# The product with w_oa in an encoder block: moved ahead of the neighbourhood attention and made of half-size products, with the modulation starting behind it

## The chip, the cores and the metric

The kernel runs on one core of one Trainium2 chip. The metric is the time of one execution on the device in microseconds; smaller is better. TensorE is called PE in the profile, VectorE DVE, ScalarE ACT, GpSimd POOL and SyncE SP. The three engines ACT, POOL and SP also start DMA transfers, each from a queue of its own that runs in order.

## The reference, cut to what matters

One layer over 512 tokens of 2048 features, all in float32:

```
mod = SiLU(c) @ w_ada + b_ada            # six vectors of 2048: shift, scale, gate, twice
h   = RMSNorm(x) * (1 + scale1) + shift1
[qA,kA,vA,qB,kB,vB,gA,gB] = h @ w_in
yA  = global attention (8 heads of 128)  # on qA, kA, vA
yB  = neighbourhood attention (8 heads)  # on qB, kB, vB
m   = sigmoid(gA) * (yA @ w_oa) + sigmoid(gB) * (yB @ w_ob)
x   = x + gate1 * (m @ w_out)
x   = x + gate2 * SwiGLU(RMSNorm(x) * (1 + scale2) + shift2)
out = RMSNorm(x)
```

w_oa and w_ob are 1024 x 2048, w_out is 2048 x 2048, w_ada is 2048 x 12288.

## The kernel before

**Split products.** Every float32 operand of a matmul is split in a high and a low half: ACT copies the high half (L163), DVE subtracts it for the low half (L165). `mm3` then issues three matmuls (L183 high x high, L184 high x low, L185 low x high). A *unit* is a weight tile of 128 x 1024 (512 KB): SP loads it into one of four `raw` buffers (L190), the two halves go to one of three `whl` buffers, and 24 matmuls with 512 columns consume it. So the loads and the splits can run up to three or four units ahead of PE.

**Two shapes of product.** `form1` (L235) computes a product with the features on the partitions, two blocks of 128 features at a time; w_in's gates, w_oa and w_ob go through it. `form2` (L249) does it with tokens on the partitions, as for the values. After each unit both call `pump` (L211), which runs due functions, one function of the list `later`, and as many steps of the background list `bg` as the current pace says.

**The modulation in the background.** The products with w_ada that only the second half of the layer needs are computed on DVE: POOL loads a tile `mw` of 128 x 1024 into one of three buffers (L335, `fetch`), and DVE multiplies it by a value of c for each partition and adds it to `acc` (L355 for the first of 16 tiles, L357 for the others). One tile is one step of `bg`. 112 tiles go this way. After 16 of them two row products on PE (bank Y and T) sum over the partitions, and DVE copies the row out (L378).

**The order around the change.** Gate A (`sg_a`) is done first; the global attention `att_a` of heads 4 to 7 (softmax chain on DVE and ACT, four transposes into bank T at L714, split pt, product into bank Y, `keep_y` stores y by ACT's queue, L684 and L685) is filled with the matmuls of the next product in program order, which is gate B, heads 0 to 8. With `p_a` released, `p_w` is taken and the modulation starts beside gate B at one step per unit. Then comes the neighbourhood attention (`att_b`) with its v, q and k, then the rest of gate B, during which `attended` loads and splits the sixteen y, one per unit (`yr`, by SP). Last comes the loop over eight pairs of feature blocks: the product of yA with w_oa (two units), evacuated by `gated` (L847, times the gate loaded by SP; for the first twelve of `sg_a` the sigmoid is taken here), the product with w_ob (two units), the sum (L859) and the split into `mT`, which w_out takes. The list `paces` gives each unit of this loop its modulation steps.

**Seven products for eight.** `group7` computes a 2 x 2 block product with seven half-size products in place of eight: the weights are loaded as two tiles, four sums of 128 x 512 are formed on DVE (`wforms`, L1008 to L1011), and four splits give the halves of seven combinations; 256 columns per matmul; seven banks are combined on DVE at the end. Before the change it is used in the feed-forward part only, with the pool `wq` adding one `raw` and two `whl` buffers.

## Time and profile before

| | us |
|---|---|
| runs (3): median, lowest, highest | 2488.75, 2488.61, 2493.84 |
| profiled execution, its own time | 2481.72 |
| span of the profiled execution | 2480.0 |
| PE busy in the span | 2449.8 (99%) |
| DVE busy | 1883.9 (76%) |
| ACT busy | 1027.6 (41%) |
| heads 4 to 7 of the global attention, with gate B's first matmuls | about 365 to 412 |
| first load of the modulation | 412.6 |
| loads of the sixteen y | about 781 to 826 |

The span runs from the first to the last instruction; the execution's own time is 1.72 us longer. In a row of a view the columns are the start, the duration, the engine, the line, the operation, the tile written and the tiles read, and in brackets how long the engine had been idle before and what ended that. In the views by stretch, each engine's busy time stands with the number of its instructions, then PE's granted clock, then the mean busy share of the DMA engines and the rate in GB/s.

### The profile page before, as it was taken

What the parts mean: (1) busy time and instruction counts of PE and PEld (TensorE: products, weight loads), DVE (VectorE), ACT (ScalarE), POOL (GpSimd) and SP (SyncE); (2) the same over time, 40 slices, a digit from 0 to 9 for tenths busy, and PEclk for the clock granted to TensorE, in tenths of its full rate; (3) what the DMA queues carried; (4) which work ended last, traced back from release to release, by engine and by line L of the source; (5) the groups of instructions that cost most, each with busy time, mean ns of one, the idle gap of its engine ahead of it and who ended that gap; (6) DMA issues with size and microseconds to landing.
All of it is one profiled execution on the core that took longest, in us unless ns stands there. A gap on an engine that the chain in (4) does not pass through costs nothing.

```text
span 2480.0 us, 40653 instructions
## 1 busy us (share of the span) xinstructions
PE 2449.8 (99%) x16607; PEld 2270.1 (92%) x16607; DVE 1883.9 (76%) x2511; ACT 1027.6 (41%) x1424; POOL 151.0 (6%) x254
## 2 busy tenths in 40 slices
PE   8999999999999999999999999999999999999998
PEld 7888888888888888888999999999999998999997
DVE  8995776556566577566898888888888885787877
ACT  5223544224334333236744444444444454434333
POOL 0100000111011111011000000000000000000010
PEclk9999999999999999999999999999999999999999
DMA  9864234865655877676353343433433456547563
GB/s 362 296 245 156 81 102 135 273 203 184 191 187 195 300 252 264 233 266 229 111 170 117 122 130 127 136 125 112 132 128 129 135 187 227 190 141 242 192 243 127
DMA packets 217466, 457.46 MB, mean 184 GB/s; under 512 B 15056, under 2 KB 68672, under 8 KB 208832
## 3 DMA queue, kind: packets, MB, share of 16 engines
q1 hardware_dynamic: 179872, 308.19, 37.6%
q0 software_dynamic: 29728, 132.20, 15.2%
q10 hardware_dynamic: 7680, 14.48, 1.6%
q8 instruction: 130, 2.13, 0.3%
q14 instruction: 56, 0.46, 0.1%
HBM read 410.74 MB, written 44.07 MB: 183 GB/s over the span
## 4 chain that ended last, share of the span: by engine, by line
PE 82%; DVE 9%; DMA 4%; issue 2%; ACT 1%; DVEq 0%; POOL 0%; ACTq 0%; POOLq 0%
PE mm L185 18%; PE mm L184 18%; PE mm L183 17%; PE S L183 6%; PE S L184 6%; PE S L185 6%; PE Y L183 3%; PE Y L184 3%; PE Y L185 3%; DVE raw L492 2%; DVE whl L165 2%; DMA raw<-in_w_down 1%; DMA yr<-y 1%; PE T L185 1%; PE T L183 1%
## 5 line engine op out<-in xcount | busy, mean ns | idle before, releaser
L163 ACT ACTIVATE whl<-raw 128x1024 fp32r<-128x1024 f32 (+1 forms) x483 | 462.0, 960 | 758.5 <-PE mm L185 376.5
L165 DVE TENSOR_TENSOR whl<-raw,whl 128x1024 fp32r<-128x1024 f32 (+1 forms) x483 | 531.2, 1109 | 255.5 <-ACT whl L163 255.1
L165 DVE TENSOR_TENSOR whl<-ta,whl 128x1024 fp32r<-128x1024 f32 x104 | 127.2, 1223 | 66.4 <-ACT whl L163 66.4
L357 DVE SCALAR_TENSOR_TENSOR acc<-mw,cact,acc 128x1024 f32<-128x1024 f32 x124 | 158.4, 1278 | 18.8 <-DMA mw<-in_ada_w 14.0
L163 ACT ACTIVATE whl<-tb 128x1024 fp32r<-128x1024 f32 x104 | 110.4, 1061 | 149.6 <-PE S L185 120.1
L163 ACT ACTIVATE whl<-ta 128x1024 fp32r<-128x1024 f32 x104 | 110.1, 1059 | 144.8 <-PE mm L185 113.9
L165 DVE TENSOR_TENSOR whl<-tb,whl 128x1024 fp32r<-128x1024 f32 x104 | 127.0, 1221 | 4.6 <-ACT whl L163 3.6
L335 POOL DMA_DIRECT2D mw<-in_ada_w x112 | 59.8, 534 | 681.7 <-DVE acc L357 384.1
L1008 DVE TENSOR_TENSOR ta<-raw 128x512 f32<-128x512 f32 x104 | 71.8, 690 | 31.5 <-DMA raw<-in_w_down 29.3
L1009 DVE TENSOR_TENSOR ta<-raw,ta 128x512 f32<-128x512 f32 x104 | 71.6, 688 | 28.0 <-DMA raw<-in_w_down 24.9
L183 PE MATMUL mm<-x56h,whl 128*128 128x256 f32 x336 | 92.4, 275 | 0.0
L184 PE MATMUL mm<-x56l,whl 128*128 128x256 f32 x336 | 92.4, 275 | 0.0
L185 PE MATMUL mm<-x56h,whl 128*128 128x256 f32 x336 | 92.4, 275 | 0.0
L183 PE MATMUL mm<-whl,s 128*128 128x256 f32 x320 | 88.1, 275 | 0.0
L183 PE MATMUL mm<-x3h,whl 128*128 128x256 f32 x320 | 88.0, 275 | 0.0
L184 PE MATMUL mm<-x3l,whl 128*128 128x256 f32 x320 | 88.0, 275 | 0.0
L185 PE MATMUL mm<-x3h,whl 128*128 128x256 f32 x320 | 88.0, 275 | 0.0
L183 PE MATMUL S<-x56h,whl 128*128 128x256 f32 x320 | 88.0, 275 | 0.0
L184 PE MATMUL S<-x56l,whl 128*128 128x256 f32 x320 | 88.0, 275 | 0.0
L185 PE MATMUL S<-x56h,whl 128*128 128x256 f32 x320 | 88.0, 275 | 0.0
L184 PE MATMUL mm<-whl,s 128*128 128x256 f32 x320 | 88.0, 275 | 0.0
L185 PE MATMUL mm<-whl,s 128*128 128x256 f32 x320 | 88.0, 275 | 0.0
(1603 smaller groups left out, 8574.4 us busy)
## 6 DMA issues: line engine op xcount, KB each, us to landing
raw<-in_w_in SPq DMA_DIRECT2D x133, 512.0 KB, 4.4
mw<-in_ada_w POOLq DMA_DIRECT2D x112, 512.0 KB, 4.9
raw<-in_w_gate SPq DMA_DIRECT2D x92, 512.0 KB, 3.6
raw<-in_w_up SPq DMA_DIRECT2D x88, 512.0 KB, 3.6
raw<-in_w_down SPq DMA_DIRECT2D x88, 512.0 KB, 5.2
raw<-in_ada_w POOLq DMA_DIRECT2D x29, 1024.0 KB, 7.0
raw<-in_w_out SPq DMA_DIRECT2D x48, 512.0 KB, 5.1
ffd<-c SPq DMA_DIRECT2D x10, 1024.0 KB, 4.8
```

Source lines behind the costliest of these rows:

```text
L163: high = pin(S.activation(hi, src, AF.Copy))
L165: latest[:] = [high, pin(eng.tensor_sub(lo, src, hi))]
L183: nc.tensor.matmul(o, lh, rh, start=start, stop=False, **kw)
L184: nc.tensor.matmul(o, lh, rl, start=False, stop=False, **kw)
L185: nc.tensor.matmul(o, ll, rh, start=False, stop=stop, **kw)
L335: mod["queue"].dma_start(w, ada2_w[n * P:(n + 1) * P, :])
L357: behind(V.scalar_tensor_tensor(acc, part, cact[:, k:k + 1], acc, op0=ALU.mult, op1=ALU.add))
L492: V.scalar_tensor_tensor(raw, raw, 1.0, call, op0=ALU.mult, op1=ALU.mult, accum_out=y)
L1008: V.tensor_sub(t1, b12, b11)
L1009: V.tensor_sub(t2_, b22, t1)
```

## The change

w_oa leaves the last loop. Behind heads 4 to 7 the pool `p_o` is taken (one more `raw` buffer and one more `whl`; the FFN's pool still has one and two). `yforms` makes the token side of the seven products for y0 to y3 and for y4 to y7: eight loads by SP into `raw` buffers, and for each of the two, four sums and four splits. It is run by the first two pumps. Then, four times, two blocks of gate B are followed by one `merged_a`: `group7` over both halves of the depth, for 512 features, times the gate (whose four loads go through POOL and whose sigmoid is taken on the whole 128 x 2048 tile), the result stored to DRAM by POOL. In the last loop the result is loaded by SP (`ma`) and the product with w_ob added to it. Only eight y are loaded and split there. `p_w`, and with it the first `mw`, comes when `p_o` is given back, behind the fourth group; no step of the modulation runs beside the first eight blocks of gate B. The modulation has a list of its own, `mods`, and each product is given its steps: two per unit in the values of `att_b`, 1, 2, 1, 2 in its q and k, one per unit in the rest of gate B, two in the first eight units of the w_ob loop, none in its last eight. The order of tokens inside a stream becomes that of 256-token blocks throughout (`MERGED`, and `mm3`'s last argument). `wforms` and `group7` are moved up in the file without a change.

```diff
-MERGED = stream_order(T)
-LAST = MERGED[stream_order(T // 2)]
+MERGED = stream_order(T // 2)
+LAST = MERGED[MERGED]
...
-        for _ in range(pace["steps"]):
-            advance()
+        advance(bg)
+        for _ in range(steps):
+            advance(mods)
...
-                        mm3(bs[j], hi[:, kk, sl], lo[:, kk, sl], xh, xl, k0 + kk == 0, k0 + kk == n - 1, T)
-                pump()
+                        mm3(bs[j], hi[:, kk, sl], lo[:, kk, sl], xh, xl, k0 + kk == 0, k0 + kk == n - 1, 256)
+                pump(next(steps))
...
     p_a.release()
     p_q.release()
+    wq = tc.alloc_tile_pool(name="p_o", bufs=1, side="right", reuse_waits="tile")
+    more_buffers(1, 1)
+    ya = {}
+    ma_d = [dram.tile([P, 2048], F32, name=f"mad{n}") for n in range(4)]
+    quarters = lambda t: t.rearrange("p (a t q n) -> p a t q n", a=2, t=2, q=2)
+
+    def yforms(s):
+
+        e, o = (raw_tile("ye") for _ in range(2))
+        for a, r in enumerate((e, o)):
+            for q in range(2):
+                nc.sync.dma_start(half(r)[:, :, q], y_d[4 * s + 2 * a + q].rearrange("p (t n) -> p t n", t=2))
+        sa = wq.tile([P, 1024], F32, tag="ta", name="sa", bufs=2)
+        sb = wq.tile([P, 1024], F32, tag="tb", name="sb", bufs=1)
+        a11, a21, a12, a22 = e[:, :512], e[:, 512:], o[:, :512], o[:, 512:]
+        V.tensor_add(sa[:, :512], a21, a22)
+        V.tensor_sub(sa[:, 512:], sa[:, :512], a11)
+        V.tensor_sub(sb[:, :512], a11, a21)
+        V.tensor_sub(sb[:, 512:], a12, sa[:, 512:])
+        ya[s] = {}
+        for src, n, rs in ((a11, 512, (1,)), (o, 1024, (2, 4)), (sa, 1024, (5, 6)), (sb, 1024, (7, 3))):
+            hl = pair(wq, f"y{s}{rs[0]}", n, 1)
+            split(*hl, src)
+            for i, r in enumerate(rs):
+                ya[s][r] = tuple(t[:, i * 512:(i + 1) * 512].rearrange("p (q n) -> p q n", q=2) for t in hl)
+
+    def merged_a(n):
+
+        c, g = (wq.tile([P, 2048], F32, tag=t, name=t, bufs=1) for t in "cg")
+        v, gv = quarters(c), quarters(g)
+        for f in range(4):
+            nc.gpsimd.dma_start(gv[:, f // 2, :, f % 2], sg_a[4 * n + f].rearrange("p (t n) -> p t n", t=2))
+        if n < 3:
+            S.activation(g, g, AF.Sigmoid)
+        group7(lambda s: wforms(w_oa, 4 * s, n * 512), ya, (0, 1), ((v[:, 0, 0], v[:, 1, 0]), (v[:, 0, 1], v[:, 1, 1])))
+        for a in range(2):
+            sl = slice(a * 1024, (a + 1) * 1024)
+            V.tensor_mul(c[:, sl], c[:, sl], g[:, sl])
+        nc.gpsimd.dma_start(ma_d[n], c)
+
+    later.extend(functools.partial(yforms, s) for s in range(2))
+    for n in range(4):
+        gates(sg_b, GB, 2 * n, 2 * n + 2)
+        merged_a(n)
+    wq.release()
...
     p_w = tc.alloc_tile_pool(name="p_w", bufs=1, side="right")
     mod["pool"] = p_w
-    bg.extend(ada_mod(k, (s2, b_sc2, n2, t2, b_sh2)) for k in range(0, KT, 4))
+    mods.extend(ada_mod(k, (s2, b_sc2, n2, t2, b_sh2)) for k in range(0, KT, 4))
...
-    gates(sg_b, GB, 0, 8)
...
-    yT = [pair(p_y, f"y{k}", T, 1) for k in range(KT)]
+    yT = [pair(p_y, f"y{k}", T, 1) for k in range(8)]
...
-    paces.extend([2, 1, 1, 1, 1, 1, 1] * 4 + [0] * 4 + [0] * 2 + [1] * 16)
+    steps = itertools.chain([2] * 8, [0] * 10, [1] * 16, itertools.repeat(0))
     for j in range(0, KT, 2):
         ma, mb = [], []
-        for w, ys, sg, to in ((w_oa, yT[:8], sg_a, ma), (w_ob, yT[8:], sg_b, mb)):
-            tag = next(turn)
-            form1([w], j * P, 2, ys, [[bank(tag), bank(tag)]], gated(sg[j:], to))
+        for e in range(2):
+            ma.append(p_y.tile([P, T], F32, tag="ma", name="ma", bufs=4))
+            a, q = divmod((j + e) % 4, 2)
+            nc.sync.dma_start(ma[e].rearrange("p (t n) -> p t n", t=2), quarters(ma_d[j // 4])[:, a, :, q])
+        tag = next(turn)
+        form1([w_ob], j * P, 2, yT, [[bank(tag), bank(tag)]], gated(sg_b[j:], mb), steps)
```

What this makes of the order on DVE. The first place is the end of the global attention and the start of gate B. `ptl` is the low half of the attention's transposed weights, the last of them that of head 7; `whl` from `raw` is the low half of a unit; `acc` from `mw` is a modulation step. Before:

```order
L165 TENSOR_TENSOR ptl_3641<-T_3655,pth_3640 128x4x128
L165 TENSOR_TENSOR ptl_3641<-T_3675,pth_3640 128x4x128
L165 TENSOR_TENSOR whl_3910<-raw_3908,whl_3910 128x1024
L355 TENSOR_SCALAR acc_3762<-mw_3763,cact_103 128x1024
L357 SCALAR_TENSOR_TENSOR acc_3762<-mw_3765,cact_103,acc_3762 128x1024
L357 SCALAR_TENSOR_TENSOR acc_3762<-mw_3767,cact_103,acc_3762 128x1024
L357 SCALAR_TENSOR_TENSOR acc_3762<-mw_3770,cact_103,acc_3762 128x1024
L165 TENSOR_TENSOR whl_3942<-raw_3940,whl_3942 128x1024
L357 SCALAR_TENSOR_TENSOR acc_3762<-mw_3802,cact_103,acc_3762 128x1024
L165 TENSOR_TENSOR whl_3974<-raw_3972,whl_3974 128x1024
L357 SCALAR_TENSOR_TENSOR acc_3762<-mw_3834,cact_103,acc_3762 128x1024
L357 SCALAR_TENSOR_TENSOR acc_3762<-mw_3866,cact_103,acc_3762 128x1024
```

The modulation's steps stood there, between the low halves of gate B's first units. After the change the same stretch (behind the last `ptl`, the low half `whl_3837` of the unit that holds h8 to h11, and two sums) reads as follows; `sa`, `sb` and the tiles that start with `y` belong to `yforms`, and `whl_3866` holds h12 to h15:

```order
L887 TENSOR_TENSOR sa_3756<-sa_3756,ye_3750 128x512
L169 TENSOR_TENSOR y01l_3763<-ye_3750,y01h_3762 128x512
L889 TENSOR_TENSOR sb_3757<-ye_3751,sa_3756 128x512
L169 TENSOR_TENSOR y02l_3767<-ye_3751,y02h_3766 128x1024
L169 TENSOR_TENSOR y05l_3771<-sa_3756,y05h_3770 128x1024
L169 TENSOR_TENSOR y07l_3775<-sb_3757,y07h_3774 128x1024
L169 TENSOR_TENSOR y11l_3820<-ye_3807,y11h_3819 128x512
L886 TENSOR_TENSOR sa_3813<-ye_3807,ye_3808 128x512
L888 TENSOR_TENSOR sb_3814<-ye_3807 128x512
L887 TENSOR_TENSOR sa_3813<-sa_3813,ye_3807 128x512
L169 TENSOR_TENSOR whl_3866<-raw_3864,whl_3866 128x1024
```

The modulation is gone from here, and the token side of the seven products stands between the low halves of gate B's third and fourth unit. Behind `whl_3866` follow the rest of `yforms` and the first sums of w_oa's weights.

The second place is the modulation's new start, behind the fourth group, in the first values of the neighbourhood attention. `c` times `g` is that group's last work on DVE; `whl_5371` belongs to the fourth unit of the values, `whl_5441` to the sixth:

```order
L908 TENSOR_TENSOR c_4985<-c_4985,g_4986 128x1024 x2
L169 TENSOR_TENSOR whl_5371<-raw_5369,whl_5371 128x1024
L169 TENSOR_TENSOR whl_5406<-raw_5404,whl_5406 128x1024
L360 TENSOR_SCALAR acc_5286<-mw_5287,cact_103 128x1024
L362 SCALAR_TENSOR_TENSOR acc_5286<-mw_5289,cact_103,acc_5286 128x1024
L362 SCALAR_TENSOR_TENSOR acc_5286<-mw_5291,cact_103,acc_5286 128x1024
L169 TENSOR_TENSOR whl_5441<-raw_5439,whl_5441 128x1024
L362 SCALAR_TENSOR_TENSOR acc_5286<-mw_5294,cact_103,acc_5286 128x1024
L362 SCALAR_TENSOR_TENSOR acc_5286<-mw_5297,cact_103,acc_5286 128x1024
L362 SCALAR_TENSOR_TENSOR acc_5286<-mw_5329,cact_103,acc_5286 128x1024
L169 TENSOR_TENSOR whl_5476<-raw_5474,whl_5476 128x1024
L362 SCALAR_TENSOR_TENSOR acc_5286<-mw_5332,cact_103,acc_5286 128x1024
```

Before, one to three steps stood between two low halves at the modulation's start, as the first fence shows; now there are three ahead of each low half from the sixth unit on.

The third place is the last loop. `o` is a product with the gate (L847 before, L1024 after), the sum with it L859 before and L1039 after, `m0l` to `m2l` are low halves of the merged result. Before, at the start of the loop:

```order
L847 TENSOR_TENSOR o_7492<-g_7490,mm_7417 128x512
L847 TENSOR_TENSOR o_7496<-g_7494,mm_7418 128x512
L859 TENSOR_TENSOR o_7410<-o_7410,o_7492 128x512
L859 TENSOR_TENSOR o_7415<-o_7415,o_7496 128x512
L165 TENSOR_TENSOR accl_7449<-acc_6709,acch_7448 128x512
L357 SCALAR_TENSOR_TENSOR acc_7362<-mw_7366,cact_103,acc_7362 128x1024
L165 TENSOR_TENSOR m0l_7316<-o_7410,m0h_7315 128x2x256
L357 SCALAR_TENSOR_TENSOR acc_7362<-mw_7369,cact_103,acc_7362 128x1024
L165 TENSOR_TENSOR m0l_7316<-o_7415,m0h_7315 128x2x256
L357 SCALAR_TENSOR_TENSOR acc_7362<-mw_7405,cact_103,acc_7362 128x1024
L165 TENSOR_TENSOR whl_7587<-raw_7585,whl_7587 128x1024
L378 COPY ada_o_7614<-Y_7484 1x512
```

After the change, ahead of the low half of the loop's eighth unit, `whl_8700` (`S_8567` and `S_8568` are the two banks that its fifth and sixth unit fill):

```order
L1024 TENSOR_TENSOR o_8644<-g_8642,S_8567 128x512
L362 SCALAR_TENSOR_TENSOR acc_8404<-mw_8544,cact_103,acc_8404 128x1024
L1024 TENSOR_TENSOR o_8648<-g_8646,S_8568 128x512
L362 SCALAR_TENSOR_TENSOR acc_8404<-mw_8547,cact_103,acc_8404 128x1024
L1039 TENSOR_TENSOR ma_8563<-ma_8563,o_8644 128x512
L362 SCALAR_TENSOR_TENSOR acc_8404<-mw_8602,cact_103,acc_8404 128x1024
L169 TENSOR_TENSOR m2l_8358<-ma_8563,m2h_8357 128x2x256
L1039 TENSOR_TENSOR ma_8565<-ma_8565,o_8648 128x512
L362 SCALAR_TENSOR_TENSOR acc_8404<-mw_8605,cact_103,acc_8404 128x1024
L169 TENSOR_TENSOR m2l_8358<-ma_8565,m2h_8357 128x2x256
L362 SCALAR_TENSOR_TENSOR acc_8404<-mw_8637,cact_103,acc_8404 128x1024
L169 TENSOR_TENSOR whl_8700<-raw_8698,whl_8700 128x1024
```

Where three steps stood among the sums of a pair of blocks, five stand now among the last of them, and five more between these and the low half of the sixth unit.

More of the change, by code (lines that the diff above doesn't have):

```diff
@@ L204, in encoder_block, with pump @@
     soon = []
-    pace = {"steps": 1}
-    paces = []
-    def pump():
-        if paces:
-            pace["steps"] = paces.pop(0)
+    mods = []
+    def pump(steps=0):
         due = [f for n, f in soon if n <= 0]
@@ L259, in form2 @@
                     mm3(banks[i], xh[:, sl], xl[:, sl], hi[:, kk], lo[:, kk], k0 + kk == 0, k0 + kk == n - 1, 256)
-            pump()
+            pump(next(steps))
         for i in tiles:
@@ L810, in encoder_block @@
-    p_b.release()
-    p_y = tc.alloc_tile_pool(name="p_y", bufs=1, side="right", reuse_waits="tile")
-    yT = [pair(p_y, f"y{k}", T, 1) for k in range(KT)]
-    def attended(h):
-        yr = raw_tile("yr")[:, :T]
-        nc.sync.dma_start(yr, y_d[h])
-        split(*yT[h], yr)
-    later.extend(functools.partial(attended, h) for h in range(KT))
-    gates(sg_b, GB, 8, KT)
-    p_h.release()
+            form1([w_in], base + j * P, 2, hT, [[bank("mm"), bank("mm")]], keep_gate(dst[j:]), itertools.repeat(steps))
@@ L866, in encoder_block @@
-    p_y.release()
-    p_w.release()
-    aside.release()
-    taken.update({t: -1 - taken[t] for t in ("raw", "whl")})
-    wq = tc.alloc_tile_pool(name="wq", bufs=1, side="right", reuse_waits="tile")
-    x2_d = dram.tile([T, D], F32, name="x2d")
-    p_w = tc.alloc_tile_pool(name="p_w2", bufs=1, side="left", reuse_waits="tile")
-    mod.update(pool=p_w, queue=nc.sync, end=128)
-    p_r = tc.alloc_tile_pool(name="p_r", bufs=1, side="right", reuse_waits="tile")
-    gate = p_r.tile([P, D], F32, name="gate1")
@@ new lines, in values @@
+    def values():
+        for i in range(NT):
+            v = st(F32R)
+            vA.append((v[:, :256], v[:, 256:]))
+            split(*vA[i], kv[i][:, 256:])
+            if i % 2:
+                yield
+    vA = []
+    q = pair(p_a, "q", 4 * T, 1)
+    bg.extend([normed(kv, 2, nw["k"], kT), normed(q_acc, 4, nw["q"], q), values()])
+    q1 = [st(F32) for _ in range(NT)]
+    form2(w_in, QA + 512, hT, lambda i, b: S.activation(q1[i], b, AF.Copy))
+    flush()
+    y_d = [dram.tile([P, T], F32, name=f"y{h}") for h in range(16)]
@@ new lines, in encoder_block, with attended, __init__, __getitem__ @@
+    p_b.release()
+    p_y = tc.alloc_tile_pool(name="p_y", bufs=1, side="right", reuse_waits="tile")
+    yT = [pair(p_y, f"y{k}", T, 1) for k in range(8)]
+    def attended(h):
+        yr = raw_tile("yr")[:, :T]
+        nc.sync.dma_start(yr, y_d[8 + h])
+        split(*yT[h], yr)
+    later.extend(functools.partial(attended, h) for h in range(8))
+    gates(sg_b, GB, 8, KT, 1)
+    p_h.release()
+    class Tokens:
+        def __init__(self, t):
+            self.t = t
+        def __getitem__(self, ix):
+            t, c = divmod(ix[1].start // P, 2)
+            return self.t[:, t, c * P:(c + 1) * P]
@@ new lines, in encoder_block, with gated, evac @@
+    p_m = tc.alloc_tile_pool(name="p_m", bufs=1, side="left")
+    mx = [pair(p_m, f"m{j}", 1024, 1) for j in range(KT // 2)]
+    mT = [tuple(Tokens(half(t)[:, :, k % 2]) for t in mx[k // 2]) for k in range(KT)]
+    def gated(src, dst):
+        def evac(w, j, b):
+            g = io.tile([P, T], F32, tag="io", name="g")
+            nc.sync.dma_start(g, src[j])
+            o = p_y.tile([P, T], F32, tag="o", name="o", bufs=4)
+            V.tensor_mul(o, g, b)
+            dst.append(o)
+        return evac
@@ new lines, in encoder_block @@
+    p_y.release()
+    p_w.release()
+    aside.release()
+    more_buffers(1, 2)
+    wq = tc.alloc_tile_pool(name="wq", bufs=1, side="right", reuse_waits="tile")
+    x2_d = dram.tile([T, D], F32, name="x2d")
+    p_w = tc.alloc_tile_pool(name="p_w2", bufs=1, side="left", reuse_waits="tile")
+    mod.update(pool=p_w, queue=nc.sync, end=128)
+    p_r = tc.alloc_tile_pool(name="p_r", bufs=1, side="right", reuse_waits="tile")
+    gate = p_r.tile([P, D], F32, name="gate1")
+    xc = {cc: p_r.tile([P, NT, 512], F32, tag=f"x{cc}", name=f"x{cc}") for cc in (3, 2)}
@@ new lines, in encoder_block, with load_x @@
+    xn = [None, None, xc[2], p_r.tile([P, NT, 512], F32, tag="n3", name="n3")]
+    xc.update({cc: p_r.tile([P, NT, 512], F32, tag=f"x{cc}", name=f"x{cc}") for cc in (0, 1)})
+    xn[:2] = xc[0], xc[1]
+    sq2 = [small.tile([P, 4], F32, tag=f"sq{i}", name=f"sq{i}", bufs=1) for i in range(NT)]
+    x3d = xp.rearrange("(i p) d -> p i d", p=P)
+    def load_x(cc):
+        if cc == 0:
+            rows(gate, g1_d)
+        nc.sync.dma_start(xc[cc], x3d[:, :, cc * 512:(cc + 1) * 512])
+    for cc in range(4):
+        later.extend([lambda: None] * (2 if cc == 0 else 3))
+        later.append(functools.partial(load_x, cc))
@@ L1096, in encoder_block, with first_half @@
+    def first_half():
+        for _ in range(4):
+            yield
+        for s in range(4):
+            for a in range(2):
+                h2_part(s, a, 0)
+                yield
+    for cc in range(2):
+        w_out_pass(cc, range(NT))
+    for cc in (2, 3):
+        w_out_pass(cc, (0, 1))
+    flush()
+    norm((0, 1))
+    bg.append(first_half())
+    for cc in (2, 3):
+        w_out_pass(cc, (2, 3))
+    flush()
+    norm((2, 3))
+    p_w.release()
     wbufs["at"] = 16
```

508 lines of the change are left out of this document (223 added, 285 removed).

## Prediction

> **What bounds the kernel now.** I read the page's totals first, then the clock and the chain.
>
> ```profile
> span 2480.0 us, 40653 instructions
> PE 2449.8 (99%) x16607; PEld 2270.1 (92%) x16607; DVE 1883.9 (76%) x2511; ACT 1027.6 (41%) x1424; POOL 151.0 (6%) x254
> PEclk9999999999999999999999999999999999999999
> PE 82%; DVE 9%; DMA 4%; issue 2%; ACT 1%; DVEq 0%; POOL 0%; ACTq 0%; POOLq 0%
> ```
>
> TensorE is busy 99% of the span, at a full clock. So the change can gain in two ways, by giving PE less to do or by closing the few gaps it has, and it can lose in one: by making PE wait. VectorE is at 76% on average, so a local heap of its work can be what PE waits for. Averages do not show that. I therefore read the stretches that the change touches, with two plain stretches beside them.
>
> ```profile
> core 0: us, PE busy (x) PEld busy (x) DVE busy (x) ACT busy (x) POOL busy (x), PEclk, DMA share, GB/s
> 365.00:412.00 47.00, 47.00 (x284) 38.61 (x283) 35.27 (x84) 28.15 (x58) 0.00 (x0) 1.00 0.19 65
> 412.00:432.00 20.00, 19.68 (x92) 16.95 (x91) 9.64 (x9) 6.25 (x7) 4.31 (x9) 1.00 0.87 292
> 780.00:830.00 50.00, 48.31 (x221) 41.29 (x221) 34.01 (x37) 20.18 (x27) 10.41 (x18) 1.00 0.95 325
> 900.00:1000.00 100.00, 100.00 (x465) 87.50 (x464) 73.69 (x83) 31.64 (x41) 10.03 (x19) 1.00 0.75 255
> 1300.00:1400.00 100.00, 100.00 (x898) 100.00 (x898) 86.40 (x109) 45.28 (x49) 0.00 (x0) 1.00 0.38 122
> 2460.00:2480.00 20.00, 9.83 (x58) 8.75 (x56) 12.02 (x32) 5.30 (x17) 0.00 (x0) 0.83 0.32 105
> ```
>
> The first row is the global attention of heads 4 to 7, filled with gate matmuls: PE has no gap. The second is the start of the modulation (0.32 us idle), the third the loads of the sixteen y (1.69 us idle), the fourth the loop of w_oa and w_ob (none). The last two give a stretch of half-size matmuls and the kernel's end.
>
> **What the change saves.** In 900 to 1000, 465 matmuls of 512 columns took 100 us: 215 ns each. In 1300 to 1400, 898 of 256 columns took 100 us: 111.4 ns. w_oa was 16 units of 24 = 384 of the first kind, 82.6 us; it becomes 4 groups x 2 x 7 x 2 x 2 x 3 = 672 of the second, 74.8 us. That saves 7.8 us. The attention and gate matmuls keep their number and widths. The idle time of rows two and three, 2.0 us, goes too if nothing takes its place: half the y loads leave the crowded stretch, and no modulation starts at gate B any more. Together -9.8.
>
> **What VectorE's pieces take.** The rates come from how closely instructions start on one another, in a row of VectorE's work in the old w_oa/w_ob loop.
>
> ```profile
> 959.45 1.28 DVE L847 TENSOR_TENSOR o<-g,mm 128x512 f32<-128x512 f32 x2
> 960.64 1.29 DVE L859 TENSOR_TENSOR o<-o 128x512 f32<-128x512 f32 x2
> 961.84 1.28 DVE L357 SCALAR_TENSOR_TENSOR acc<-mw,cact,acc 128x1024 f32<-128x1024 f32 x1
> 963.04 1.29 DVE L165 TENSOR_TENSOR m4l<-o,m4h 128x512 fp32r<-128x512 f32 x2
> 964.24 1.28 DVE L357 SCALAR_TENSOR_TENSOR acc<-mw,cact,acc 128x1024 f32<-128x1024 f32 x1
> 965.44 1.22 DVE L165 TENSOR_TENSOR whl<-raw,whl 128x1024 fp32r<-128x1024 f32 x1
> ...
> 972.98 1.22 DVE L165 TENSOR_TENSOR whl<-raw,whl 128x1024 fp32r<-128x1024 f32 x1
> 974.11 1.28 DVE L357 SCALAR_TENSOR_TENSOR acc<-mw,cact,acc 128x1024 f32<-128x1024 f32 x1
> ```
>
> Two operations of 512 columns start 1.19 us before the next row, so one is 0.60; a modulation step is 1.20 (961.84 to 963.04); the low half of a unit, on which PE's third product waits, is 1.13 (972.98 to 974.11). A unit is 24 matmuls x 0.215 = 5.16 us of PE.
>
> **A: the start of w_oa.** The gate's fill in heads 4 to 7 shrinks from 75 matmuls (the first twelve and a half h) to 48 (h0 to h7), since the unit of h8 now stands behind the attention. What remains must follow the softmax chain:
>
> ```profile
> 404.49 0.66 PE L714 MATMUL T<-ident,e 128*128 128x128 f32 x4
> 406.56 0.66 PE L714 MATMUL T<-ident,e 128*128 128x128 f32 x4
> 408.62 0.66 PE L714 MATMUL T<-ident,e 128*128 128x128 f32 x4
> 409.95 0.69 DVE L165 TENSOR_TENSOR ptl<-T,pth 128x512 fp32r<-128x512 f32 x1 [1.38 <-ACT pth L163]
> ```
>
> The transposes stand 2.06 us apart and VectorE waits for each, so 27 matmuls (5.8 us) taken from between them do not shorten the tail by 5.8: I take half, 2.9 us of idle (0 to 5.8). Then VectorE's new order decides. Between the last ptl and the first low half of w_oa's forms stand, one by one: the low half of h8's unit (1.13), five sums and splits of 512 columns and three of 1024 (3.0 + 3.4), four more of 512 (2.4), the low half of h12's unit (1.13), one sum and three splits (0.6 + 3.4), three sums and one split of 512 (2.4). Sum 17.5 us. PE has in that time the last head's 12 products (1.3) and two units (10.3), 11.6 us, and may put three or four high products first (0.4). Gap 5.5 us. It falls mostly ahead of h12's unit: about 10 us of VectorE against one unit of PE. Two transfers lengthen it:
>
> ```profile
> y<-yo ACTq DMA_DIRECT2D x16, 256.0 KB, 2.2
> yr<-y SPq DMA_DIRECT2D x16, 256.0 KB, 4.6
> raw<-in_w_oa SPq DMA_DIRECT2D x16, 512.0 KB, 5.5
> raw<-in_w_in SPq DMA_DIRECT2D x133, 512.0 KB, 4.4
> accd<-acc POOLq DMA_DIRECT2D x8, 1024.0 KB, 6.5
> ffd<-c POOLq DMA_DIRECT2D x1, 1024.0 KB, 4.4
> ```
>
> On SP the weights of h8's unit are queued behind the load of y6, which waits until y6 is stored; 4.4 us of landing from there is about 1.5 us after the attention's end. And the sums over y4 to y7 need y7 stored (2.2) and loaded (4.6) first, about as late as VectorE gets there (0.6 more). 2.9 + 5.5 + 1.5 + 0.6: A = 10.5 us, from 5.5 (VectorE's count alone) to 15.
>
> **B: the modulation's new start.** Its pool is taken only when the last w_oa group is in DRAM. So the first mw waits for: the last sum and the two products with the gate (some 4 us after PE's last matmul of the group), the 1 MB store (4.4 to 6.5 in the rows above), and its own landing:
>
> ```profile
> 412.60 1.08 POOL L335 DMA_DIRECT2D mw<-in_ada_w  x2 [251.51 <-PE Y L185]
> 419.28 0.75 DVE L355 TENSOR_SCALAR acc<-mw,cact 128x1024 f32<-128x1024 f32 x1 [7.00 <-DMA mw<-in_ada_w]
> 423.06 1.28 DVE L357 SCALAR_TENSOR_TENSOR acc<-mw,cact,acc 128x1024 f32<-128x1024 f32 x1 [0.71 <-DMA mw<-in_ada_w]
> 447.92 1.28 DVE L357 SCALAR_TENSOR_TENSOR acc<-mw,cact,acc 128x1024 f32<-128x1024 f32 x1 [0.87 <-DMA mw<-in_ada_w]
> ```
>
> 6.7 from issue to use: 16 us after the group. By then PE is in the fourth unit of the first v. VectorE's order has three steps ahead of each of six low halves (sixth unit of v to the third of q and k). The sixth is done at 16 + 3.8 + 1.2 + 1.1 = 22.1; PE asks at 5 x 5.16 = 25.8, so 3.7 in hand. Then each unit needs three mw. From 419.28 to 447.92 twelve steps started, 2.60 us apart and waiting for DMA: 7.8 per unit. By bandwidth alone, three mw and one weight tile of 0.52 MB at the 325 GB/s of 780 to 830 take 6.5. Against PE's 5.16 that is 1.3 to 2.6 lost in each of five units, 6.5 to 13.2, less 3.7: 2.8 to 9.5. At 7.1, B = 6; 0 if mw keeps up, as at the old pace of one a unit.
>
> **C: the w_ob loop.** Two steps per unit for eight units. Ahead of the low half of the loop's eighth unit (whl_8700 of the order) stand ten steps, eight gate products and sums, five splits and a copy: with the seventh unit's own low half 22.7 us between those of whl_8609 and whl_8700, the sixth and the eighth. The first of these reads a bank that PE finishes with the fourth unit, and PE asks for whl_8700's low half three units and eight high products later: 15.5 + 1.7 = 17.2. Gap 5.5. The order has a harder point within: the product that reads bank S can start only when PE ends the sixth unit; 10.8 us of VectorE follow up to the low half, and PE has 6.9 (one unit and eight products) for it: 3.9 at the least. If the ten mw come 2.60 apart, 26 - 17.2 = 8.8. C = 6 (3.9 to 8.8).
>
> **D: the rest.** Sigmoid, 1 MB store and half-MB loads lie off the path; the denser steps beside the neighbourhood attention may cost 1 us (0 to 4). Token blocks of 256 change no count.
>
> **Sum.** -7.8 - 2.0 + 10.5 + 6 + 6 + 1 = +13.7 us. The profiled execution took 2481.72 us, 7 below the median of 2488.75; to the median it gives 2502, in the trace 2495. About 0.2%, 5 us, is what a measurement of this kernel can tell from no change.
>
> **A rule against the change.** The 2460 to 2480 row is the only one here with a clock below 1.00, 0.83, and PE is idle for 10 of its 20 us. If A's and C's gaps of about 5 us each did the same, a fall of 0.17 over 20 us would be 3.4 us each, 6.8 together: 2509. The Trainium skill ("TensorE: Matmul & The Clock Gate", Part 1: The HAM clock gate) has the clock halve after an idle window of about 3.4 us and return after as long a busy one; by that, an estimate, each such gap would cost up to 1.7 us more, 3.4 in all. The rows of before have no inner gap of that length to test it.
>
> **The rivals.**
> 1. *Faster: the queues stay in hand.* The row at 959.45 shows a heap of 6 us on VectorE in front of a low half, while 900 to 1000 has no PE idle: split buffers held the lead. If that also holds at h12's unit, PE loses only the tail's 2.9: -9.8 + 2.9 = -6.9, 2481.9. It decides at whether h12's low half is ready 5.2 us after h8's; against it stand 10 us of VectorE in that order.
> 2. *No change: A alone.* B and C are swallowed since mw lands ahead of need: -9.8 + 10.5 = +0.7, 2489.5. For it: DMA share 0.19 before this place. Against: 2.60 us per mw.
> 3. *Slower still: the clock falls in the gaps*, 2509 as above, or all bounds at their upper end.
>
> **Chances.** Forecast 0.54, first rival 0.22, second 0.14, third 0.10. So faster 0.22, within 0.2% 0.14, slower 0.64. The range runs from 2480 (first rival's end) to 2513 (the third and the upper bounds, short of all at once); the forecast's own runs from 2495 to 2511, since its four unknown terms (12.2 to 37.3 together, less 9.8) will hardly all lie at one end.
>
> **What would show it.** Right: PE idle some 10 us around 409 to 430, waiting for the low half of h12's unit and then of the first form; idle in the first q and k units with VectorE behind mw; one gap at the seventh unit of w_ob; 672 matmuls of 256 columns at 111 ns. Wrong: PE busy without gaps in 405 to 430, or VectorE found waiting for PE, not the reverse, at those three places.

## The result and the profile after

The changed kernel takes 2520.48 us (median of 5 runs, 2516.12 to 2525.44) against 2488.75 for the kernel before (5 runs, 2484.94 to 2493.84). The ratio is 1.0127 with a 95% interval of 1.0113 to 1.0142: slower by 31.7 us, where 13.7 were forecast and 2513 was the upper end of the range. The direction was right, the size was not.

The page after, in its totals, the clock and the chain that ended last:

```profile
span 2519.3 us, 41396 instructions
PE 2455.9 (97%) x16895; PEld 2280.7 (91%) x16895; DVE 1943.5 (77%) x2587; ACT 1044.3 (41%) x1435; POOL 164.6 (7%) x274
PEclk9999999998999999999999999999999999999999
PE 67%; DVE 13%; issue 9%; DMA 7%; ACT 2%; POOL 0%; DVEq 0%; SPq 0%; POOLq 0%; ACTq 0%
```

The span grew by 39.3 us in the profiled executions (the one of before was at the quick end of its runs). PE's idle time, span less busy time, grew from 30.2 to 63.4, by 33.2. Its busy time grew as well, by 6.1, although its work shrank. PE's share of the chain fell from 82% to 67%, and VectorE, DMA and issue took it.

The stretches in which this happened, with the stretch of the four groups (440 to 570) among them:

```profile
core 0: us, PE busy (x) PEld busy (x) DVE busy (x) ACT busy (x) POOL busy (x), PEclk, DMA share, GB/s
400.00:440.00 40.00, 31.48 (x194) 26.97 (x193) 32.67 (x47) 25.35 (x34) 2.88 (x4) 0.91 0.67 216
440.00:570.00 130.00, 129.97 (x883) 121.58 (x882) 83.73 (x99) 47.35 (x52) 10.19 (x15) 1.00 0.50 168
600.00:640.00 40.00, 28.34 (x120) 23.95 (x119) 27.25 (x26) 7.86 (x10) 7.48 (x14) 0.83 0.85 293
880.00:920.00 40.00, 37.38 (x165) 31.83 (x165) 27.47 (x32) 15.11 (x20) 7.82 (x14) 0.96 0.97 345
980.00:1020.00 40.00, 33.30 (x145) 28.50 (x144) 33.90 (x40) 9.83 (x14) 5.79 (x11) 0.91 0.80 263
1080.00:1120.00 40.00, 36.46 (x157) 31.18 (x156) 20.39 (x18) 9.97 (x15) 6.02 (x4) 0.91 0.88 293
```

The groups themselves run without a gap: once begun, they are what they should be. Around them are five places where PE waits, and in each the granted clock falls too. PE's timeline gives every wait of over 0.45 us between 340 and 1220, with the idle time and its releaser in brackets:

```profile
402.86 0.65 PE L850 MATMUL T<-ident,e 128*128 128x128 f32 x4 [0.60 <-DVE ptl L169]
404.20 0.38 PE L187 MATMUL Y<-pth,st 128*128 128x256 f32 x1 [0.69 <-ACT pth L167]
408.34 0.38 PE L187 MATMUL Y<-pth,st 128*128 128x256 f32 x1 [0.69 <-ACT pth L167]
418.81 0.48 PE L187 MATMUL mm<-h12h,whl 128*128 128x512 f32 x1 [2.81 <-ACT whl L167]
422.79 1.22 PE L189 MATMUL mm<-h12h,whl 128*128 128x512 f32 x2 [2.85 <-DVE whl L169]
620.41 0.80 PE L187 MATMUL mm<-h0h,whl 128*128 128x512 f32 x1 [11.65 <-DVE vl L169]
898.38 0.50 PE L379 MATMUL T<-acch,ones_r 128*128 128x512 f32 x1 [2.39 <-ACT acch L167]
1003.68 1.22 PE L189 MATMUL mm<-y4h,whl 128*128 128x512 f32 x2 [6.70 <-DVE whl L169]
1098.17 0.80 PE L187 MATMUL mm<-whl,m0h 128*128 128x512 f32 x1 [3.54 <-DVE ro L1078]
```

They sum to 31.9 us. The first five are A, the sixth is B, the eighth C; the seventh (beside the rest of gate B) and the ninth (the first pass of w_out) had no term in the forecast.

The other part is the clock. Behind the wait of B, PE's timeline reads:

```profile
621.00 0.63 PE L188 MATMUL mm<-h0l,whl 128*128 128x512 f32 x1
621.43 0.63 PE L189 MATMUL mm<-h0h,whl 128*128 128x512 f32 x1
...
625.27 0.60 PE L189 MATMUL mm<-h1h,whl 128*128 128x512 f32 x1
625.70 0.39 PE L187 MATMUL mm<-h2h,whl 128*128 128x512 f32 x1
```

Up to 625.87 the matmuls start 0.43 us apart, afterwards 0.22: half the clock for 5.5 us, 2.7 us lost. Behind the other four places the chain shows the same step for 5.1 us (from 422.8), 3.3 (899.1), 4.5 (1003.7) and 5.7 (1098.2), so 2.5, 1.6, 2.3 and 2.9 us. Together 12.0 us. With the 7.8 us that w_oa saves, PE's busy time should grow by 4.2; it grew by 6.1, and the last 1.9 us are spread too thinly to place.

### The profile page after: what moved, and what is told of

Its sections match the earlier page's. It is cut to its first block, busy times and chain, and to the rows that moved or that the text cites. A ratio compares the mean times of both kernels' runs of the same rounds, so it can differ in the third digit from the quotient of the medians.

```text
span 2519.3 us, 41396 instructions
## 1 busy us (share of the span) xinstructions
PE 2455.9 (97%) x16895; PEld 2280.7 (91%) x16895; DVE 1943.5 (77%) x2587; ACT 1044.3 (41%) x1435; POOL 164.6 (7%) x274
## 4 chain that ended last, share of the span: by engine, by line
PE 67%; DVE 13%; issue 9%; DMA 7%; ACT 2%; POOL 0%; DVEq 0%; SPq 0%; POOLq 0%; ACTq 0%
PE mm L189 15%; PE mm L188 15%; PE mm L187 15%; PE S L187 4%; PE S L189 4%; PE S L188 4%; DVE whl L169 3%; PE Y L187 2%; PE Y L188 2%; PE Y L189 2%; DVE raw L497 2%; DMA raw<-in_w_down 2%; DMA mw<-in_ada_w 2%; DVE acc L362 1%; DMA raw<-in_w_out 1%
## 5 line engine op out<-in xcount | busy, mean ns | idle before, releaser
L169 DVE TENSOR_TENSOR whl<-raw,whl 128x1024 fp32r<-128x1024 f32 (+1 forms) x483 | 525.3, 1098 | 199.2 <-ACT whl L167 198.9
L169 DVE TENSOR_TENSOR whl<-ta,whl 128x1024 fp32r<-128x1024 f32 x112 | 136.8, 1222 | 85.9 <-ACT whl L167 85.8
L167 ACT ACTIVATE whl<-ta 128x1024 fp32r<-128x1024 f32 x112 | 118.6, 1059 | 156.8 <-PE mm L189 116.5
L167 ACT ACTIVATE whl<-tb 128x1024 fp32r<-128x1024 f32 x112 | 118.5, 1058 | 156.9 <-PE S L189 118.3
L169 DVE TENSOR_TENSOR whl<-tb,whl 128x1024 fp32r<-128x1024 f32 x112 | 136.6, 1219 | 14.0 <-ACT whl L167 13.0
L667 DVE TENSOR_TENSOR ta<-raw 128x512 f32<-128x512 f32 x112 | 77.2, 689 | 40.4 <-DMA raw<-in_w_down 30.5
L668 DVE TENSOR_TENSOR ta<-raw,ta 128x512 f32<-128x512 f32 x112 | 77.0, 687 | 32.4 <-DMA raw<-in_w_down 28.5
L669 DVE TENSOR_TENSOR tb<-raw 128x512 f32<-128x512 f32 x112 | 77.0, 687 | 3.2 <-DMA raw<-in_w_down 1.3
```

What stands on the lines that cost most here:

```text
L167: high = pin(S.activation(hi, src, AF.Copy))
L169: latest[:] = [high, pin(eng.tensor_sub(lo, src, hi))]
L667: V.tensor_sub(t1, b12, b11)
L668: V.tensor_sub(t2_, b22, t1)
L669: V.tensor_sub(t3, b22, b12)
```

## The experiments

Each line of results gives the median, the ratio to the kernel before and its interval. The kernel before ran beside each of them, at medians of 2486.55 to 2488.43.

**e1_spread: the first place.**

```diff
-    later.extend(functools.partial(yforms, s) for s in range(2))
-    for n in range(4):
-        gates(sg_b, GB, 2 * n, 2 * n + 2)
+    pause = [lambda: None] * 2
+    later.extend(pause + [functools.partial(yforms, 0)] + pause + [functools.partial(yforms, 1)])
+    for n, (j0, j1) in enumerate(((0, 4), (4, 6), (6, 8), (8, 8))):
+        gates(sg_b, GB, j0, j1)
         merged_a(n)
```

> Two pairs of gate B stand ahead of the first group instead of one, the two parts of the token side are run at the third and the sixth unit, and the last two groups follow each other. Theory (separate waits, each with a stretch of half clock behind it): PE's 8.5 us of idle between 402 and 423 and the 2.5 us of half clock behind them go, less up to 3 us where two groups follow each other without a gate between: 2509 to 2513 us, PE busy without a gap over 1 us before the first group. Rival (one heap of work on VectorE and the DMA engines that only moves): the gap comes back at the first group or behind the last, 2517 us or more.

Measured: 2504.34 us, 1.0077 (1.0055 to 1.0098), 16 us less by the medians and more than the 7.5 to 11.5 expected. In PE's timeline one wait is left ahead of the first group, and the clock stays at 1.00 behind it:

```profile
433.51 0.48 PE L189 MATMUL mm<-h12h,whl 128*128 128x512 f32 x1 [2.22 <-DVE whl L169]
```

The waits of the attention's tail are gone too, as more gate matmuls are at hand to fill it. Up to the first values nothing came in their place, so the theory of separate waits holds here. The profiled execution is the slowest of the four (2511.88); in it the row product beside the rest of gate B waited 4.10 us, not 2.39, and the last two groups run without a gap.

**e2_v0: no step beside the first values.**

```diff
-        form2(w_in, VB + hh * 512, hT, lambda i, b: split(*v[i], b), steps=itertools.repeat(2))
+        form2(w_in, VB + hh * 512, hT, lambda i, b: split(*v[i], b), steps=itertools.repeat(2 if hh else 0))
...
-            form1([w_in], QB + h0 * HD, 2, hT, [[bank("mm"), bank("mm")]], lambda w, j, b: queries(*qs[j], b), iter((1, 2, 1, 2)))
+            form1([w_in], QB + h0 * HD, 2, hT, [[bank("mm"), bank("mm")]], lambda w, j, b: queries(*qs[j], b), itertools.repeat(2))
```

The same for k, and `fetch()` as soon as the pool is there.

> No modulation step beside the first values of the neighbourhood attention (0 in place of 2 per unit), two per unit in all q and k, the first three tiles asked for as soon as the pool is there. Theory of separate waits: the wait of 11.65 us for the evacuation of the first values and the 2.7 us of half clock behind it go, the steps find room beside q and k: 2506 us, 2505 to 2510. Rival of one heap: the same steps are only later, and PE waits as long in q and k: 2516 us or more.

Measured: 2527.58 us, 1.0158 (1.0135 to 1.0181), no better than the change. The 11.65 us are gone, but three waits stand in their place in PE's timeline:

```profile
707.91 0.38 PE L188 MATMUL S<-kl,qh 128*128 128x256 f32 x1 [3.44 <-DVE kl L169]
763.15 0.80 PE L187 MATMUL mm<-h0h,whl 128*128 128x512 f32 x1 [4.86 <-DVE vl L169]
813.64 0.58 PE L188 MATMUL S<-kl,qh 128*128 128x256 f32 x1 [4.52 <-DVE kl L169]
```

12.8 us, the last two with half clock behind them, and the time lies 17 us above the range that the theory gave. Here the theory fell: B is not a wait that can be taken out by itself. Steps moved within the neighbourhood attention take their wait along.

**e3_ob1: the w_ob loop.**

```diff
-    steps = itertools.chain([2] * 8, [0] * 10, [1] * 16, itertools.repeat(0))
+    steps = itertools.chain([1, 1, 2] * 4, [0] * 6, [1] * 16, itertools.repeat(0))
```

> In the w_ob loop the sixteen steps are spread over twelve units (1, 1, 2) in place of eight (2). Theory of separate waits: the 6.7 us of idle at the loop's eighth unit and 2.3 us of half clock go: 2511 us, 2510 to 2514. Rival of one heap: the wait comes later in the loop or in w_out, 2517 us or more.

Measured: 2508.89 us, 1.0086 (1.0066 to 1.0106). The 6.70 us at the loop's eighth unit became 2.09 with no fall of the clock. The wait in w_out went from 3.54 to 0.96, but that it hung on this loop is not shown: with the loop of the changed kernel it was 1.07 in e2_v0 and 1.45 in e11_fill.

**e4_late: the modulation moved, w_oa left where it was.** The kernel before, with these edits (and the modulation's two lines behind gate B's first half):

```diff
+    paces.extend(([2] * 8 + [1, 2] * 8) * 2 + [1] * 16)
...
-    paces.extend([2, 1, 1, 1, 1, 1, 1] * 4 + [0] * 4 + [0] * 2 + [1] * 16)
+    paces.extend([2] * 8 + [0] * 26 + [1] * 16)
```

> The kernel before, with the modulation alone moved: no step beside the first eight blocks of gate B, then two per unit in the values, 1, 2, 1, 2 in q and k, two per unit for eight units of the last loop, as in the changed kernel; w_oa stays in the last loop. Theory: the late and dense modulation makes B and C by itself, weaker since its first tile needs no store ahead of it: 4 to 16 us slower than before, 2493 to 2505, with a gap at the end of the first values. Rival (w_oa's groups, their loads and stores make the gaps): within 3 us of before.

Measured: 2489.45 us, 1.0004 (0.9991 to 1.0017): no difference, and not the 4 to 16 us that my theory gave. The same pace of steps from the first values to the rest of gate B costs nothing here (in the last loop it covers two pairs of feature blocks, as w_oa's units are among its eight, where the changed kernel's covers four). The difference is seen in VectorE's timeline, in the first step of the modulation and the first of the second sum of sixteen:

```profile
474.54 0.75 DVE L355 TENSOR_SCALAR acc<-mw,cact 128x1024 f32<-128x1024 f32 x1
...
515.98 0.75 DVE L355 TENSOR_SCALAR acc<-mw,cact 128x1024 f32<-128x1024 f32 x1
```

The first tiles are asked for at 416, long ahead; the steps begin 8 us before the values do (482.5) and keep ahead of PE; sixteen are done by 516, before the values are to be evacuated (copied out of their banks by ACT and DVE) at 523. So a late start in program order does no harm by itself. Something that e4_late lacks does.

**e5_comb: e1_spread and e3_ob1 together**, with both of their diffs.

> The edits of e1_spread (token side spread, two pairs of gate B ahead of the first group) and of e3_ob1 (sixteen steps over twelve units of the w_ob loop) together. If their waits are separate, the gains add: 2520.5 - 16.1 - 11.6 = 2493 us, 2490 to 2496. If they share a cause, the sum is less than the parts: 2498 us or more.

Measured: 2501.25 us, 1.0047 (1.0029 to 1.0066). The median lies above the 2490 to 2496 expected of separate waits, on the side of the rival. The seven runs fall in two groups, three of 2493.87 to 2496.37 and four of 2501.25 to 2503.86, so the time does not decide: by the ratios the two edits took 0.0050 and 0.0041 of the 0.0127, which leaves 1.0036, and that lies in the interval. The trace (an execution of 2496.37) does: the wait ahead of the first group is 2.54 us, the one in the w_ob loop 2.38, and neither edit's wait came back elsewhere. So A and C are separate, and B is still there (11.92 us).

**e6_tile: the pool's wait.**

```diff
-    p_w = tc.alloc_tile_pool(name="p_w", bufs=1, side="right")
+    p_w = tc.alloc_tile_pool(name="p_w", bufs=1, side="right", reuse_waits="tile")
```

> One word: the modulation's pool waits only for those tiles of w_oa's pool whose place it takes, and not for all of the pool. Theory (B comes from the first tile's late start, 16 us into the first values, so that sixteen steps end behind the values): the first step comes 3 to 6 us earlier, the wait of 11.65 us shrinks by as much, 5 to 9 us in place of it, 2513 to 2518 us. Rival (B comes from the density of the steps, three ahead of each low half): the wait stays at 10 us or more, 2518 us or more.

Measured: 2517.21 us, 1.0125 (1.0103 to 1.0147). The experiment decides nothing, since the first step hardly came earlier: 15.7 us after the values began, against 16.7 in the changed kernel. On POOL:

```profile
573.90 0.56 POOL L909 DMA_DIRECT2D mad<-c  x1 [29.80 <-DVE c L908]
578.72 1.70 POOL L340 DMA_DIRECT2D mw<-in_ada_w  x3 [4.26 <-issue]
```

The loads of mw still stood behind the last group's store, 4.8 us after it. The wait of B was 10.99 us.

**e7_best: e5_comb, the pool's wait of e6_tile, first tiles asked for at once, eight steps fewer in the first values and eight more beside the rest of gate B.**

```diff
-        form2(w_in, VB + hh * 512, hT, lambda i, b: split(*v[i], b), steps=itertools.repeat(2))
+        form2(w_in, VB + hh * 512, hT, lambda i, b: split(*v[i], b), steps=itertools.repeat(2 if hh else 1))
...
-    gates(sg_b, GB, 8, KT, 1)
+    gates(sg_b, GB, 8, KT, itertools.cycle((1, 2)))
```

> e5_comb's edits, the pool's earlier start of e6_tile with the first three tiles asked for at once, one step per unit in the first values, and the eight steps saved there put beside the rest of gate B (1, 2). Theory of separate waits: e5_comb's time less all of B (11.65 and 2.7): 2479 us, 2477 to 2485, faster than before. Rival: the eight steps bring a wait beside the rest of gate B, where the row product already waited for 2.4 us, and the time stays at 2486 or more.

Measured: 2499.34 us, 1.0049 (1.0034 to 1.0064). No wait is left at the first values; 2.67 us at a k, 4.40 at the second values and 4.49 beside the rest of gate B came for it. Again the wait moved, and the time is 14 us above the range of the theory.

**e8_late16: e4_late with the changed kernel's order in the first values.**

```diff
-    paces.extend(([2] * 8 + [1, 2] * 8) * 2 + [1] * 16)
+    paces.extend([0, 0, 0, 4, 3, 3, 3, 3] + [1, 2] * 8 + [2] * 8 + [1, 2] * 8 + [1] * 16)
```

> The kernel before with the modulation moved as in e4_late, and in the first values its sixteen steps in the last five units (0, 0, 0, 4, 3, 3, 3, 3), which gives VectorE the changed kernel's order: three steps ahead of each low half from the fifth unit on. The pool is free early, so the first three tiles are there in time. Theory (late first tile): without the store ahead of the first tile the density costs 0 to 6 us: 2488 to 2494. Rival (density): a wait of 8 us or more at the end of the first values, 2498 us or more.

Measured: 2498.29 us, 1.0048 (1.0034 to 1.0061), 4 us over the range of the theory and at the lower end of the rival's, with this wait, smaller than the rival's, in PE's timeline:

```profile
529.99 0.80 PE L183 MATMUL mm<-h0h,whl 128*128 128x512 f32 x1 [6.26 <-DVE vl L165]
```

VectorE's row of the first low half of the values, for which PE waits:

```profile
529.25 0.69 DVE L165 TENSOR_TENSOR vl<-mm,vh 128x512 fp32r<-128x512 f32 x1
```

The first tiles are early here, and still PE waits, for half as long. With e4_late this says what decides: when the steps are done that stand ahead of this low half in VectorE's order. They start at 489.28, 7.6 us after the values begin; the seventeenth stands at 525.65, 36.4 us later, the eighteenth at 528.05; the values are over at 523.7. In the changed kernel they start 16.7 us after the values begin, and seventeen stand ahead.

**e9_phase: e5_comb with twelve steps in the first values and four more in its q and k**, and the pool's wait and the early first tiles of e7_best.

```diff
-        form2(w_in, VB + hh * 512, hT, lambda i, b: split(*v[i], b), steps=itertools.repeat(2))
+        form2(w_in, VB + hh * 512, hT, lambda i, b: split(*v[i], b), steps=itertools.repeat(2) if hh else iter((1, 1, 1, 1, 2, 2, 2, 2)))
```

> e5_comb with the first tiles asked for at once, twelve steps in place of sixteen in the first values and four more in its q and k, so that no sum of sixteen steps ends where values end. If PE waited in B because the sixteenth step and its row sum stand ahead of the evacuation of the values, the 11.9 us and the half clock behind them go: 2484 to 2488 us. If it is the number of steps in this stretch (80 beside 48 units, limited by DMA), gaps of 2 us and more stand at the evacuation of k or of the second values: 2493 us or more.

Measured: 2501.17 us, 1.0059 (1.0042 to 1.0076). A wait of 8.36 us stays at the end of the first values. On VectorE sixteen steps (574.00 to 608.62) still stand ahead of the first low half, although the values have only twelve; the copy and the low half of a sum stand there no longer. So the end of a sum is not the cause; the steps that VectorE takes ahead of the evacuation are.

**e10_defer: e5_comb with one step per unit in both values, and the sixteen saved in w_out.** The pool's wait and the early first tiles are those of e7_best, and w_out's first load of x comes two units later.

```diff
-    mod = {"pool": None, "queue": nc.gpsimd, "next": 0, "end": 112}
+    mod = {"pool": None, "queue": nc.gpsimd, "next": 0, "end": 96}
...
-        form2(w_in, VB + hh * 512, hT, lambda i, b: split(*v[i], b), steps=itertools.repeat(2))
+        form2(w_in, VB + hh * 512, hT, lambda i, b: split(*v[i], b), steps=itertools.repeat(1))
...
-    steps = itertools.chain([2] * 8, [0] * 10, [1] * 16, itertools.repeat(0))
+    steps = itertools.chain([1, 1, 2] * 4, [0] * 6, [1] * 32, itertools.repeat(0))
```

> e5_comb with the first tiles asked for at once, one step per unit in both values, and the sixteen steps saved put into w_out, which has 32 in place of 16 (by SP's queue). If the number of steps beside the neighbourhood attention is the cause, no gap over 1.5 us is left between 560 and 880, the half-size products' 7.8 us show, and the time is 2478 to 2485 us, at or below before. If the late start alone makes B, a gap of 4 us or more stays at the end of the first values; if w_out cannot take the steps, a gap of 3 us or more comes there: 2490 us or more.

Measured: 2495.43 us, 1.0036 (1.0021 to 1.0050), 10 us over the range given. The neighbourhood attention is as forecast, PE idle for 2.3 us of 320 in the table of stretches (e9_phase, with the same early first tiles and all 80 steps, still waited 8.36 at one place):

```profile
560.00:880.00 320.00, 317.68 (x1561) 271.54 (x1559) 218.48 (x290) 113.95 (x206) 52.37 (x93) 1.00 0.70 231
```

What is left stands elsewhere: 2.13 us ahead of the first group, 2.07 in the w_ob loop and 3.47 in w_out, each with the clock down to 0.83 over 10 us. PE's timeline at two of them:

```profile
975.20 0.70 PE L189 MATMUL mm<-y4h,whl 128*128 128x512 f32 x2 [2.07 <-DVE whl L169]
...
1159.67 0.48 PE L188 MATMUL mm<-whl,m3h 128*128 128x512 f32 x1 [3.47 <-DVE whl L169]
```

**e11_fill: work for PE in the wait of B.** The 44 matmuls add work and change no result.

```diff
+        if not hh:
+            spare = bank("S")
+            for _ in range(44):
+                behind(nc.tensor.matmul(spare, hT[0][0][:, :P], hT[0][0], start=True, stop=True))
         for hp in range(2):
```

> The changed kernel with 44 matmuls of 512 columns, whose result nobody reads, between the first values and the first q: 9.5 us of work for PE in the stretch in which it waits 11.65 us. If the wait itself lowers the clock, the first matmuls behind it then run at 0.22 us and not at 0.43, the granted clock of 610 to 630 is 1.00, and the time is 2 to 3 us below the changed kernel's. If the clock falls for another reason, it stays at about 0.6 there and the time as it was or up to 9.5 us longer.

Measured: 2518.31 us, 1.0127 (1.0110 to 1.0144). Its first matmuls of q, at the place where the changed kernel's ran at 0.43:

```profile
622.38 0.48 PE L187 MATMUL mm<-h0h,whl 128*128 128x512 f32 x1 [0.68 <-DVE vl L169]
622.70 0.38 PE L188 MATMUL mm<-h0l,whl 128*128 128x512 f32 x1
622.92 0.38 PE L189 MATMUL mm<-h0h,whl 128*128 128x512 f32 x1
```

0.22 us apart, and the granted clock of 600 to 640 is 1.00, not 0.83. PE's idleness itself lowers the clock: that is shown. The time did not show it, its interval includes the changed kernel's: the 2.7 us are about what this measurement can tell, and a wait of 1.75 us with some half clock came at 668 instead.

**e12_tuned: e10_defer with its three waits eased.**

```diff
-    later.extend(pause + [functools.partial(yforms, 0)] + pause + [functools.partial(yforms, 1)])
+    later.extend(pause + [functools.partial(yforms, 0)] + pause * 2 + [functools.partial(yforms, 1)])
...
-    steps = itertools.chain([1, 1, 2] * 4, [0] * 6, [1] * 32, itertools.repeat(0))
+    steps = itertools.chain([2, 1, 1, 1] * 3 + [1, 0, 0, 0], [0, 2] + [1] * 14 + [1, 0] * 16, itertools.repeat(0))
```

> e10_defer with its three longest waits eased: the second part of the token side runs after the eighth unit of gate B and not the sixth, the sixteen steps of the w_ob loop come 2, 1, 1, 1, and the 32 steps of w_out go to its sixteen full units and to every other of its half units. If what e10_defer lost against the 7.8 us that the half-size products save is these waits (2.1, 2.1 and 3.5 us) with the half clock behind each, they go and the time is 2480 to 2486 us, at or below before (ratio 0.996 to 0.999). If w_oa's move costs in another way too, it stays above 2488 us with no wait of 2 us or more left.

Measured: 2481.52 us (median of 12), 0.9974 (0.9963 to 0.9984): faster than both kernels, by 6.9 us against before (17 runs, 2488.43). Its page:

```profile
span 2476.3 us, 41403 instructions
PE 2443.6 (99%) x16895; PEld 2271.5 (92%) x16895; DVE 1942.2 (78%) x2587; ACT 1043.6 (42%) x1435; POOL 157.7 (6%) x258
```

No wait between 340 and 1220 is over 1.5 us, the granted clock of that stretch is 1.00, and PE's busy time is 6.2 us below before's. The half-size products' 7.8 us are real; the changed kernel hid them under 33 us more of waits and 12 of half clock.

## Why the prediction was wrong, step by step

**The saving of 7.8 us: right.** A group's 168 matmuls start 0.111 us apart, the stretch 440 to 570 has no gap, and e12_tuned shows nearly all of it.

**A, 10.5 us: right in place, in size partly by luck.** The tail's waits of 0.69 and less sum to 2.9, as forecast. Ahead of the fourth unit of gate B PE waited 2.81 + 2.85, where 5.5 and 0.6 were put. The unit of h8 was not late, so the 1.5 us for its weights fell away; 2.5 us of half clock, for which A had no term, came in its place and brought the sum back to 11. What ended last there is told by the chain of waits:

```profile
411.22 4.80 DMA y<-yo
416.04 3.64 DMA ye<-y
419.70 0.69 DVE sa L886
420.91 0.69 DVE sa L887
421.60 1.15 DVE whl L169
422.79 1.22 PE mm L189 x2
```

The round trip of y7 through DRAM took 8.4 us with VectorE's queue behind it; I had it at 6.8 and level with the count of VectorE's work.

**B, 6 us: wrong in size and in place.** The first step came 16.7 us after the values began (566.84), where 16 were put, and the steps 2.2 us apart, where 2.4 were put (7.1 for three). But the low halves of the weights, on which I let PE lose 1.3 to 2.6 us a unit, were in time: PE ran through all eight units. It stopped where I had not looked, at the evacuation of the values, whose banks q needs. VectorE and ACT have it in their rows:

```profile
583.53 0.75 DVE L360 TENSOR_SCALAR acc<-mw,cact 128x1024 f32<-128x1024 f32 x1 [3.50 <-DMA mw<-in_ada_w]
...
617.60 1.28 DVE L362 SCALAR_TENSOR_TENSOR acc<-mw,cact,acc 128x1024 f32<-128x1024 f32 x1
619.01 0.75 DVE L360 TENSOR_SCALAR acc<-mw,cact 128x1024 f32<-128x1024 f32 x1
619.68 0.68 DVE L169 TENSOR_TENSOR vl<-mm,vh 128x512 fp32r<-128x512 f32 x1
```

```profile
606.85 0.60 ACT L167 ACTIVATE vh<-mm 128x512 fp32r<-128x512 f32 x1 [2.23 <-PE mm L189]
618.91 0.63 ACT L167 ACTIVATE acch<-acc 128x512 fp32r<-128x512 f32 x1 [11.46 <-DVE acc L362]
619.45 1.55 ACT L167 ACTIVATE vh<-mm 128x512 fp32r<-128x512 f32 x3
```

On VectorE all sixteen steps and the first of the next sum (619.01) stand ahead of the low halves `vl`, and on ACT the copy of the sum (`acch`) ahead of three of the four high halves. So PE waits from 608.8 until the first `vl` is done at 620.4 and one bank is free. The condition is: start of the steps, plus the number that stand ahead of the first `vl` times 2.2 us, against the 42 us that the values take. It gives 16.7 + 17 x 2.2 for the changed kernel (12.1 late; 11.65 measured), 7.6 + 18 x 2.2 for e8_late16 (5.2 late; 6.26 measured) and, with its steps 2.3 apart, 13.7 + 16 x 2.3 for e9_phase (8.5 late; 8.36 measured), while e4_late's steps began 8 us before the values did and it has no wait. e2_v0, e7_best and e9_phase show that shifting steps between the values, q and k moves the wait, and e10_defer that it goes when sixteen of the 80 steps leave this stretch.

**C, 6 us: right.** 6.70 us, at the loop's eighth unit (the list of signs said the seventh) and by the order that was named; e3_ob1 takes all but 2.09 of it away. Half clock added 2.3.

**D, 1 us: wrong.** The row product beside the rest of gate B waited 2.39 and 0.23 us with 1.6 of half clock behind it. The chain puts a load of y ahead of it that took 9.21 us (from 886.03), on DMA engines busy at 0.97 between 880 and 920: the crowd at the y loads, whose 1.7 us I had credited as gone, was still there. That this load is the cause is read from the chain alone; no run takes it away. And w_out's first pass waited 3.54 us plus 2.9 of half clock. The chain puts a load of w_out's weights of 7.32 us (from 1086.60) ahead of it; as the wait was 1.07 to 3.54 us in runs with the same loop, its cause stays open.

**The clock: the step that failed most.** The sum put it at nothing, and the third rival, at a chance of 0.10, had two such gaps and up to 6.8 us. There were five, 12.0 us, and e11_fill shows that PE's waiting is what lowers the clock. The Trainium skill ("TensorE: Matmul & The Clock Gate", Part 1: The HAM clock gate) has the clock halve after an idle window of about 3.4 us and return after a busy one. By it I had put up to 1.7 us on each gap, as an estimate. These traces agree in the direction, but less idle time was enough (2.39 us at 898), and matmuls ran at half clock for 3.3 to 5.7 us, a loss of 1.6 to 2.9 us a gap.

By the profiled executions: 13.7 forecast against 39.3. B's wait accounts for 5.7 us more than put, the two waits that D lacked for 5.2, C for 0.7, the clock for 12.0; A's idle time was 2.0 less than put: 35.3. The 2.0 us of idle time that I had credited did come, as the other waits between 340 and 1220 fell from 3.9 to 1.8 us; but PE's gaps before 340 and behind 1220 grew by 2.4 in small pieces, and 1.9 us of busy time stay unplaced. That is 39.6, which by rounding and the two ends of the span is 0.3 over. The medians differ by 7.6 less, as the profiled execution of before was 7 us below its median; what a slower run of before loses, no trace shows.

## What to carry to other kernels

When work is moved in front of a stretch, price what is pushed behind it: list, for each engine's order, what stands ahead of the *evacuation* of a product's banks as well as of its operands. A background stream limited by DMA has a rate (here 2.2 to 2.6 us a tile); moving its start costs nothing until start plus rate times count, of the steps ahead of the first evacuation, passes the point where the next product needs the bank, and then its lateness is PE's. Count each PE wait of some 2 us or more with 1.6 to 2.9 us of half clock, and treat waits with separate causes (A and C) separately from a load that only moves (B): the second needs less work in the stretch, not another order.
